# 512-column token products with four accumulators in two mixers of a transformer kernel

## The chip, the cores and the metric

The kernel runs on one core of a Trainium2 chip. The metric is the device time of one execution in microseconds (us), lower is better. A run's time is compared with runs of the kernel before on the same chip.

## What is computed

The reference is two transformer blocks on 512 tokens of width 1024, in float32. The first block is an FFN, a mixer (mixer 1) and a second FFN; the second is a mixer (mixer 2) and an FFN with a convolution. What the change touches are column ranges of the mixers' input products. Cut to these:

```
# mixer 1: h = rms_norm(x) [512, 1024]
c_q, k_a, v_a, k_idx, w_idx, q_b, k_b, v_b, gate_a, gate_b = split(h @ w_in)
y_b = stick_breaking_attention(q_b, k_b, v_b)     # 8 heads of 64: v_b has 512 columns
# mixer 2: u = rms_norm(h)
rq, rk, rv, rgate, dq, dk, dv, dz, db, da, gate_r, gate_d = split(u @ w_in_2)
rq, rk = rotary(rq), rotary(rk) / 8               # 512 columns each
ro  = retention_chunkwise(rq, rk, rv)             # rv, rgate: 1024 columns each
y_r = (silu(rgate) * group_norm(ro)) @ w_ret_br
do  = gated_delta_chunkwise(conv(dq), conv(dk), conv(dv), ...)
merged = sigmoid(gate_r) * y_r + sigmoid(gate_d) * (gated(do, dz) @ w_dn_br)
```

## The kernel before, in words

Every large product is three float32r products: both operands are cut into a high and a low part (`mm3`, L140: lines L143, L144, L145 are its three matmuls). `wpanel` (L126) loads a panel of weights by a DMA from SP's queue (L134), rounds it on ScalarE (L135, the high part) and subtracts on VectorE (L136, the low part). Four raw panels and two pairs of high and low panels exist at a time.

There are two shapes of product. `feat_gemm` (L155) has 128 weight columns as the stationary operand and streams 512 tokens: each matmul is 128x512. `tok_gemm` (L176) has 128 tokens as the stationary operand and streams the weight columns, 256 to 272 of them: each matmul is 128x256. For 256 columns it takes two panels of 4x256, and for each of four token blocks one accumulator after another: 8 x 3 matmuls into one PSUM bank, then the evacuation. So 256 columns are 4 x 24 = 96 matmuls.

PSUM has eight banks, divided by name and divided anew by `repsum` (L1488): `mm` is what both products use. In mixer 1's projections and in mixer 2 up to the first weave's end `mm` has 4 banks; in mixer 2's third weave 3; in its end 8. With 4 or more, `feat_gemm` takes 256 columns a step, otherwise 128.

**Mixer 1.** `b_proj` (L732) makes the stick attention's queries, keys and values for a half of the heads; the values (`e_v`, L756) are one `tok_gemm` of 256 columns a half. Half 0's values stay in two slots; half 1's go to DRAM by four DMAs (L761) and `b_stick` (L775) brings them back by two (L783). A slot is one of 45 SBUF buffers of 128x512 (`slot`, L46), given out when an older one is released.

**Mixer 2.** Retention's part: `proj_r(half)` (L1252) makes for a half of the heads queries and keys, 256 columns each, evacuated through `rope` (L490: on VectorE two products L495 and L496/L497 that read PSUM, a sum on GpSimd L502, a product L503) and values, twice 256 columns, evacuated by ScalarE (L1268). All go to DRAM (`stage`, L309) and come back in `ret_chain` (L1281). `ret_fin` (L1338) makes the gate, twice 256 columns a half: Silu on ScalarE (L1347), a product on GpSimd (L1348), four normalisations (L1352) and a product (L1354) on VectorE; then `to_features` transposes.

The rest of mixer 2: `dn_first`, `dn_rest` and `dn_fin` are the delta rule, a chain of small float32 products (for half 0 and half 1), `gates(br)` (L1363) the branch gates, 1024 columns each by `feat_gemm`, `merge` (L1371) the output products.

What sets the order: `weave` (L58) traces generators step by step side by side by weights, `urgent` (L70) moves steps up in priority by so many instructions, and a scheduler in the build puts each engine's instructions in order by these priorities and a simulated time. Each engine, and SP's DMA queue, then runs in that order. Mixer 2's order is written out in L1394 to L1411:

```python
    weave((urgent(C, dn_rest(0, d0), X1), 0.5), (urgent(C, dn_first(1, d1), X2), 1.0),
          (chain(proj_r(0, r0), gates(0)), 0.15))
    C.repsum({"mm": 3, "pd": 3, "pr": 2})
    weave((urgent(C, dn_rest(1, d1), X3), 0.75),
          (chain(dn_fin(0, d0), proj_r(1, r1), gates(1)), 1.0),
          (urgent(C, chain(ret_chain(0, r0), ret_fin(0, r0)), X4), 0.5))
```

The first of these two is called the second weave below, the other the third; in each the chain without `urgent` is the fill: products that wait for nothing and stand between the links of the delta rule's chain. A fourth weave has `ret_chain(1)` and the fill `dn_fin(1)` and seven steps of `merge(0)`; `ret_fin(1)`, the last step of `merge(0)` and `merge(1)` follow.

Of the kernel before, what the change touches and what calls it, by code (L numbers as in the profile page):

```python
# [8 lines left out]
F32 = mybir.dt.float32  # L9
# [3 lines left out]
OP = mybir.AluOpType  # L13
# [3 lines left out]
P = 128  # L17
# [10 lines left out]
class Ctx:  # L28
# [29 lines left out]
def weave(*gens):  # L58
    """Traces the generators' steps side by side; each is (generator, steps it takes for one of the others)."""
# [10 lines left out]
def urgent(C, g, offset):  # L70
    """g's steps, as if traced that many instructions earlier."""
# [38 lines left out]
def load_columns(C, rows, name, pool=None):  # L110
    """rows: APs [n, 128] in DRAM; returns a [128, sum n] tile with one column for each row."""
# [14 lines left out]
def wpanel(C, w, k0, nk, c0, n):  # L126
    """w[k0*128:(k0+nk)*128, c0:c0+n] as two float32r parts whose sum is exact."""
# [12 lines left out]
def mm3(C, ps, lhs, rhs, start, stop, **kw):  # L140
    """ps += lhs^T rhs from exact float32r parts: lhs and rhs are (hi, lo)."""
# [6 lines left out]
def split(C, src, hi, lo):  # L148
    """src = hi + lo, both float32r."""
# [5 lines left out]
def feat_gemm(C, h, w, kb, c0, ncols, evac, k0=0, tokens=T):  # L155
    """evac(j, psum) for each 128 columns of w: psum = (h w[k0*128:])^T, [128 columns, tokens]."""
# [19 lines left out]
def tok_gemm(C, h, w, kb, c0, n, evac):  # L176
    """evac(tb, psum): psum[:, :n] = (h w)[128 tokens of block tb, c0:c0+n]; n in 256..272, kb 8 or less."""
# [80 lines left out]
def rsqrt_small(C, src, n, scale, eps, name, bufs=2):  # L258
    """1/sqrt(src*scale + eps) on [128, n]: exp(-ln/2), then a Newton step."""
# [39 lines left out]
def spill(C, xT):  # L299
    """x goes to DRAM while the mixer needs its room."""  # L300
# [8 lines left out]
def stage(C, t, name):  # L309
    """A slot's content goes to DRAM for a while; unstage() brings it back."""  # L310
# [11 lines left out]
def add_spilled(C, xs):  # L322
    """The evacuation that adds to the x of spill(), and the list it fills with the sums."""
# [60 lines left out]
def ffn_conv(C, xT, g, wu, wd, cw, cb, last):  # L384
    """last(xT, G, f0) as in ffn_phases(); cw[tap], cb [128, 44]: taps and bias of the 44 blocks of 128 channels."""
# [50 lines left out]
def rope_setup(C, positions, inv_freq):  # L436
    """cos, sin [128 tok, 4 blocks, 32] of the positions' angles."""
# [36 lines left out]
def rope_table(C, cs, sn, g, scale, name):  # L474
    """ct, st [128, 4, 64]: rope(y*g)*scale = y*ct + halves_swapped(y)*st."""
# [14 lines left out]
def rope(C, out, src, ct, st, n, r=None, tag="ta"):  # L490
    """out [128, n, 64] = (src*ct + swap(src)*st) * r; ct, st broadcast to [128, n, 64]; r [128, n] or None."""
# [14 lines left out]
def mixer1(C, xT, a, W):  # L506
# [33 lines left out]
    yb, qa, qi, kT = [None] * 4, [], [None], []  # L540
# [4 lines left out]
    def a_proj():  # L545
        # c_q | k_a v_a k_idx w_idx, tokens on partitions
# [35 lines left out]
        # keys: norm, rope, and transposed twice over, for both halves of the partitions  # L582
# [18 lines left out]
        # queries  # L601
# [15 lines left out]
        def q_done(i, tb, src, r):  # L617
# [8 lines left out]
            # each head's two parts, on the two halves of the partitions  # L626
# [23 lines left out]
    def a_topk():  # L650
        # the index scores' 128 largest among the causal keys; block 0 has no more than 128
# [927 lines left out]
```

## Time and profile before

| | us |
|---|---|
| median of 3 runs | 2203.46 |
| the runs | 2199.79, 2203.46, 2204.78 |
| span of the profiled execution (first to last instruction; no other time is listed for it) | 2203.8 |
| TensorE busy in it | 2162.9 (98%) |
| VectorE, ScalarE, GpSimd busy | 1236.6, 900.5, 238.2 |

The page of the profile gives the busy time of each engine, the chain of work that ended last, and groups of instructions. Matmuls overlap in the pipeline, so a matmul's duration is longer than its distance to the next one; what one costs in a stream is the distance between starts, which is read from the rows in order of time.

### The profile page before, as it was taken

Reading aid. Unit: us, or ns where it says so; the run is one execution under the profiler, and the core shown is the slowest. Engines: PE = TensorE matmul, PEld = TensorE weight load, DVE = VectorE, ACT = ScalarE, POOL = GpSimd, SP = SyncE. Lnnn points to the kernel's source line nnn. Section 1 sums busy time; section 2 is a strip of 40 time slices with the busy share of each in tenths; the row PEclk is TensorE's granted clock in tenths of the full one; section 3 lists DMA queues with packets and bytes.
Section 4 is the critical chain, followed back from the end, with each engine's and each line's share of the span. In section 5 each row is a group of like instructions: output and inputs, shape, how many; then the busy total and the mean of one; then the engine's idle time right before and its main releaser. Section 6 shows DMA issues by size and latency. Waiting matters only on the chain.

```text
span 2203.8 us, 29456 instructions
## 1 busy us (share of the span) xinstructions
PE 2162.9 (98%) x11346; PEld 1837.3 (83%) x11346; DVE 1236.6 (56%) x2268; ACT 900.5 (41%) x1554; POOL 238.2 (11%) x221
## 2 busy tenths in 40 slices
PE   8999999999999899999999999999999999999998
PEld 6888888887887788888888889899888988888887
DVE  5542434578975744333446897654546455653662
ACT  4321223356578442212334545242344344432442
POOL 1110110114100001101100000011011110210210
PEclk9999999999999999999999999999999999999999
DMA  5333335578433833333243435533343452323331
GB/s 164 96 96 96 97 95 135 96 107 122 89 96 113 261 96 97 96 98 100 89 139 118 133 99 163 165 105 103 115 157 120 139 172 88 104 95 96 96 113 60
DMA packets 268206, 254.43 MB, mean 115 GB/s; under 512 B 25927, under 2 KB 237857, under 8 KB 268065
## 3 DMA queue, kind: packets, MB, share of 16 engines
q1 hardware_dynamic: 267488, 251.49, 40.4%
q8 instruction: 89, 1.46, 0.3%
q10 hardware_dynamic: 576, 1.05, 0.1%
q14 instruction: 53, 0.43, 0.1%
HBM read 221.02 MB, written 31.47 MB: 115 GB/s over the span
## 4 chain that ended last, share of the span: by engine, by line
PE 89%; DVE 3%; ACT 3%; DMA 3%; issue 1%; POOL 0%; SPq 0%; DVEq 0%; ACTq 0%; POOLq 0%
PE mm L145 27%; PE mm L144 27%; PE mm L143 26%; DVE wlo L136 1%; DMA tb<-part 1%; PE mm L720 1%; ACT whi L135 1%; DMA g<-t 1%; PE pb L838 1%; PE pb L799 1%; PE pd L1132 0%; PE pa L701 0%; PE pr L1313 0%; PE pb L828 0%; PE mm L717 0%
## 5 line engine op out<-in xcount | busy, mean ns | idle before, releaser
L143 PE MATMUL mm<-e,whi 128*128 128x512 f32 (+1 forms) x2240 | 865.3, 387 | 6.0 <-ACT e L150 3.2
L144 PE MATMUL mm<-e,whi 128*128 128x512 f32 (+1 forms) x2240 | 860.9, 385 | 0.0
L145 PE MATMUL mm<-e,wlo 128*128 128x512 f32 (+1 forms) x2240 | 832.2, 386 | 5.9 <-DVE wlo L136 5.8
L136 DVE TENSOR_TENSOR wlo<-raw,whi 128x1024 fp32r<-128x1024 f32 (+1 forms) x369 | 430.2, 1167 | 440.1 <-ACT whi L135 421.4
L135 ACT CAST whi<-raw 128x1024 fp32r<-128x1024 f32 (+1 forms) x369 | 369.4, 1002 | 693.7 <-PE mm L144 524.7
L143 PEld LDWEIGHTS mm<-e,whi 128*128 128x128 f32 x2240 | 420.9, 188 | 91.6 <-ACT e L150 4.4
L145 PEld LDWEIGHTS mm<-e,wlo 128*128 128x128 f32 x2240 | 420.7, 188 | 91.4 <-DVE wlo L136 9.2
L144 PEld LDWEIGHTS mm<-e,whi 128*128 128x128 f32 x2240 | 421.2, 188 | 83.7 <-issue 2.3
L144 PE MATMUL mm<-wlo,e 128*128 128x256 f32 (+3 forms) x672 | 194.5, 293 | 3.0 <-DVE wlo L136 2.9
L145 PE MATMUL mm<-whi,e 128*128 128x256 f32 (+3 forms) x672 | 193.6, 292 | 0.0
L143 PE MATMUL mm<-whi,e 128*128 128x256 f32 (+3 forms) x672 | 186.4, 292 | 3.1 <-ACT td L1233 1.8
L144 PEld LDWEIGHTS mm<-wlo,e 128*128 128x128 f32 x672 | 128.7, 192 | 6.2 <-DVE wlo L136 4.4
L368 POOL TENSOR_TENSOR t<-t,rb 128x512 f32<-128x512 f32 x44 | 65.4, 1487 | 616.2 <-ACT t L367 612.9
L143 PEld LDWEIGHTS mm<-whi,e 128*128 128x128 f32 x672 | 126.6, 192 | 6.4 <-ACT whi L135 2.0
L145 PEld LDWEIGHTS mm<-whi,e 128*128 128x128 f32 x672 | 128.6, 192 | 1.6
L396 DVE SCALAR_TENSOR_TENSOR t<-t,fcw 128x511 f32<-128x511 f32 x88 | 66.1, 751 | 29.0 <-ACT t L393 27.1
L411 POOL TENSOR_TENSOR t<-t 128x512 f32<-128x512 f32 x22 | 48.9, 2222 | 305.5 <-DVE t L396 280.6
L150 ACT CAST e<-t 128x512 fp32r<-128x512 f32 x50 | 31.0, 621 | 85.9 <-DVE t L375 43.4
L144 PE MATMUL mm<-g,whi 128*128 128x512 f32 x160 | 62.4, 390 | 0.0
L143 PE MATMUL mm<-g,whi 128*128 128x512 f32 x160 | 62.3, 390 | 0.0
L145 PE MATMUL mm<-g,wlo 128*128 128x512 f32 x160 | 60.1, 391 | 0.8 <-DVE wlo L136 0.8
L334 DVE SCALAR_TENSOR_TENSOR e<-mm,e 128x512 f32<-128x512 f32 x56 | 38.4, 689 | 37.2 <-PE mm L145 37.0
(408 smaller groups left out, 2249.8 us busy)
## 6 DMA issues: line engine op xcount, KB each, us to landing
raw<-w_in SPq DMA_DIRECT2D x100, 512.0 KB, 5.0
raw<-w_up SPq DMA_DIRECT2D x88, 512.0 KB, 3.7
raw<-w_down SPq DMA_DIRECT2D x59, 512.0 KB, 3.5
raw<-w_gate SPq DMA_DIRECT2D x44, 512.0 KB, 3.9
xs<-e SPq DMA_DIRECT2D x16, 256.0 KB, 3.3
g<-t SPq DMA_DIRECT2D x16, 256.0 KB, 2.0
raw<-w_o_a SPq DMA_DIRECT2D x16, 256.0 KB, 3.3
raw<-w_out SPq DMA_DIRECT2D x8, 512.0 KB, 8.4
```

Of the source, the lines that this page charges most:

```text
L135: nc.scalar.copy(hi[:, :N], raw[:, :N])
L136: nc.vector.tensor_tensor(lo[:, :N], raw[:, :N], fl(hi[:, :N]), op=OP.subtract)
L143: nc.tensor.matmul(ps, lhs[0], rhs[0], start=start, stop=False, **kw)
L144: nc.tensor.matmul(ps, lhs[0], rhs[1], start=False, stop=False, **kw)
L145: nc.tensor.matmul(ps, lhs[1], rhs[0], start=False, stop=stop, **kw)
L150: C.nc.scalar.copy(hi, src)
L334: C.nc.vector.scalar_tensor_tensor(xT[j], ps, alpha, xT[j], op0=OP.mult, op1=OP.add)
L368: nc.gpsimd.tensor_tensor(s3, s2, nm.rb, op=OP.mult)
L396: nc.vector.scalar_tensor_tensor(y[:, n:], u[:, :T - n], cw[k][:, f:f + 1], y[:, n:], op0=OP.mult, op1=OP.add)
L411: nc.gpsimd.tensor_tensor(pr, y, act[f + j], op=OP.mult)
L720: nc.tensor.matmul(po, va[:, sb, :], pp, start=sb == 0, stop=sb == tb)
L799: nc.tensor.matmul(zs(sb)[:, u * P:(u + 1) * P], k[:, sb * P:(sb + 1) * P], q[u][:, ts], start=(sb % 2 == 0 and u == 0), stop=False, skip_ ...
```

## The change

A second token product, `tok_gemm_wide`, streams 512 weight columns a matmul. It takes panels of 2x512 and four accumulators at once: each panel is used for all four token blocks (24 matmuls), and all four accumulators end within the last panel. It replaces `tok_gemm` in three places: the stick values of mixer 1 (one product of 512 columns in `b_proj(0)`, in four slots kept for both halves, with no way through DRAM), all of retention's queries, keys and values (`proj_r()` now makes both halves at once, four products), and the gate of half 1 (`ret_fin(1)`). `ret_fin(0)` keeps two products of 256.

The fill of mixer 2 changes with it: the second weave has all of `proj_r` and the first half (two steps of 256 columns) of `gates(0)`; the third has `dn_fin(0)`, the rest of `gates(0)` and `gates(1)`. `ret_chain` loads its half of queries and keys by eight DMAs of 128x256 and its values by four of 128x512, where eight of 128x512 stood.

The diff, cut to its core (removed comments and docstrings are left out):

```diff
+def tok_gemm_wide(C, h, w, kb, c0, evac):
+    acc = [ptile(C) for _ in range(4)]
+    for kp in range(0, kb, 2):
+        wp = wpanel(C, w, kp, 2, c0, 512)
+        for tb in range(4):
+            ts = slice(tb * P, (tb + 1) * P)
+            for k in range(2):
+                mm3(C, acc[tb], (h[0][kp + k][:, ts], h[1][kp + k][:, ts]), (wp[0][:, k, :], wp[1][:, k, :]),
+                    kp + k == 0, kp + k == kb - 1)
+            if kp + 2 == kb:
+                evac(tb, acc[tb])
+    yield
...
     def b_proj(half, st):
-        v = [C.dram.tile([P, T], F32, name=f"bsv{i}") if half else slot(C) for i in range(2)]
...
         def e_v(tb, ps):
-            cols = slice(tb % 2 * 256, tb % 2 * 256 + 256)
-            t = tmp(C)[:, :256] if half else v[tb // 2][:, cols]
-            nc.scalar.activation(t, ps[:, :256], AF.Copy, scale=nm.rt[:, tb:tb + 1])
-            if half:
-                nc.sync.dma_start(v[tb // 2][:, cols], t)
+            vb.append(slot(C))
+            nc.scalar.activation(vb[tb], ps, AF.Copy, scale=nm.rt[:, tb:tb + 1])
...
-        yield from tok_gemm(C, h, w_in, 8, 1544 + half * 256, 256, e_v)
+        if half == 0:
+            yield from tok_gemm_wide(C, h, w_in, 8, 1544, e_v)
...
-    def proj_r(half, st):
+    def proj_r():
+        def put(t, name, halves=2):
+            d = C.dram.tile([P, halves, T // halves], F32, name=name)
+            nc.sync.dma_start(d, t.rearrange("p (u n) -> p u n", u=halves))
+            return d
...
+                r = small(C, 8, "rdr", 3)
+                nc.vector.tensor_scalar(r, rdec[:, i, :], nm.rt[:, tb:tb + 1], None, op0=OP.mult)
+                w = lambda t: t.rearrange("p (h d) -> p h d", d=64)
+                t = slot(C)
+                rope(C, w(t), w(ps), rct[:, tb:tb + 1, :].to_broadcast([P, 8, 64]),
+                     rst[:, tb:tb + 1, :].to_broadcast([P, 8, 64]), 8, r, "td")
+                rkept[n].append(put(t, f"st{n}{tb}"))
...
+                t = slot(C)
+                nc.scalar.activation(t, ps, AF.Copy, scale=nm.rt[:, tb:tb + 1])
+                rkept[f"v{half}"].append(stage(C, t, f"stv{half}{tb}"))
...
+            yield from tok_gemm_wide(C, h, w_in, 8, i * 512, e_qk(n, i))
+        for half in range(2):
+            yield from tok_gemm_wide(C, h, w_in, 8, 1024 + half * 512, e_v(half))
...
     def ret_chain(half, st):
-        qk = {n: [unstage(C, d) for d in st[n]] for n in "qk"}
-        vv = [[unstage(C, d) for d in st[f"v{grp}"]] for grp in range(2)]
+        qk = {n: [slot(C), slot(C)] for n in "qk"}
+        for n in "qk":
+            for tb in range(4):
+                nc.sync.dma_start(tok(n, tb), rkept[n][tb][:, half, :])
+        vv = [unstage(C, d) for d in rkept[f"v{half}"]]
...
-        for grp in range(2):
-            yield from tok_gemm(C, h, w_in, 8, 2048 + half * 512 + grp * 256, 256, e(grp))
+        if half:
+            yield from tok_gemm_wide(C, h, w_in, 8, 2048 + half * 512, e(0, 512))
+        else:
+            for grp in range(2):
+                yield from tok_gemm(C, h, w_in, 8, 2048 + half * 512 + grp * 256, 256, e(grp))
...
-    m0 = merge(0)
+    m0, g0 = merge(0), gates(0)
...
-          (chain(proj_r(0, r0), gates(0)), 0.15))
+          (chain(proj_r(), some(g0, 2)), 0.15))
     C.repsum({"mm": 3, "pd": 3, "pr": 2})
     weave((urgent(C, dn_rest(1, d1), X3), 0.75),
-          (chain(dn_fin(0, d0), proj_r(1, r1), gates(1)), 1.0),
+          (chain(dn_fin(0, d0), g0, gates(1)), 1.0),
```

## Rows read from the trace of the kernel before

**Rows 1.** The page: span, TensorE's busy time, the chain that ended last.
```profile
span 2203.8 us, 29456 instructions
...
PE 2162.9 (98%) x11346; PEld 1837.3 (83%) x11346; DVE 1236.6 (56%) x2268; ACT 900.5 (41%) x1554; POOL 238.2 (11%) x221
...
PE 89%; DVE 3%; ACT 3%; DMA 3%; issue 1%; POOL 0%; SPq 0%; DVEq 0%; ACTq 0%; POOLq 0%
```

**Rows 2.** TensorE's groups by shape (busy us, mean ns, idle before): three of them.
```profile
L143 PE MATMUL mm<-e,whi 128*128 128x512 f32 x2112 | 827.3, 392 | 3.0 <-ACT e L150 2.0 <-ACT whi L135 1.0
...
L143 PE MATMUL mm<-whi,e 128*128 128x256 f32 x576 | 159.6, 288 | 2.2 <-ACT td L1233 1.8 <-ACT whi L135 0.4
...
L145 PE MATMUL mm<-whi,g 128*128 128x512 f32 x32 | 12.5, 390 | 0.0
```

**Rows 3.** TensorE in order of time (start us, us): end of mixer 2, gate of half 1.
```profile
1687.17 0.40 PE L144 MATMUL mm<-e,whi 128*128 128x512 f32 x1
...
1709.84 0.39 PE L145 MATMUL mm<-e,wlo 128*128 128x512 f32 x1
1710.07 0.28 PE L143 MATMUL mm<-whi,e 128*128 128x256 f32 x1
...
1721.46 0.28 PE L145 MATMUL mm<-whi,e 128*128 128x256 f32 x1
```

**Rows 4.** TensorE's waits over 150 ns from 1310 to 1550 us (total, times, longest).
```profile
PE mm L144 <- DVE wlo L136: 1.4, 3, 0.7
...
PE mm L143 <- ACT whi L135: 0.4, 1, 0.4
```

**Rows 5.** VectorE and GpSimd by shape: the rope's instructions, mixer 1, eight heads.
```profile
L503 DVE TENSOR_TENSOR ta<-ta,rq 128x512 f32<-128x512 f32 x4 | 2.8, 693 | 0.8 <-POOL ta L502 0.6
...
L495 DVE TENSOR_TENSOR ta<-pa,tic 128x512 f32<-128x512 f32 x3 | 2.1, 692 | 6.1 <-PE pa L145 6.1
...
L496 DVE TENSOR_TENSOR ta<-pa,tis 128x256 f32<-128x256 f32 x3 | 1.2, 415 | 0.0
...
L502 POOL TENSOR_TENSOR ta<-ta 128x512 f32<-128x512 f32 x4 | 6.0, 1504 | 25.7 <-DVE ta L497 25.7
```

**Rows 6.** VectorE by shape, 1310 to 1550 us: the panel splits.
```profile
L136 DVE TENSOR_TENSOR wlo<-raw,whi 128x1024 fp32r<-128x1024 f32 x30 | 36.6, 1220 | 16.6 <-DMA e<-ret_norm_g 9.4 <-ACT whi L135 7.0
```

**Rows 7.** Busy time by stretch: us, PE, PEld, DVE, ACT, POOL, clock, DMA.
```profile
1310.00:1450.00 140.00, 137.70 (x1009) 126.11 (x1008) 99.69 (x270) 55.48 (x153) 9.97 (x17) 1.00 0.53 155
1450.00:1640.00 190.00, 187.62 (x1386) 174.16 (x1385) 96.16 (x223) 65.71 (x122) 24.01 (x30) 1.00 0.39 118
```

**Rows 8.** ScalarE by shape: a copy of 512 columns out of PSUM.
```profile
L639 ACT COPY ya<-pa 128x512 f32<-128x512 f32 x4 | 2.3, 583 | 1.1 <-PE pa L145 1.1
```

**Rows 9.** The delta rule's first and last product by half (first to last start).
```profile
L1124 PE MATMUL pd<-dw x32: 271/275/347, 1322.9 to 1399.9; 128*128 128x128 f32 x32
...
L1180 PE MATMUL pd<-td,dw x32: 270/275/276, 1367.3 to 1444.5; 128*128 128x128 f32 x32
...
L1124 PE MATMUL pd<-dw x32: 273/275/276, 1458.4 to 1588.9; 128*128 128x128 f32 x32
...
L1180 PE MATMUL pd<-td,dw x32: 270/275/276, 1551.2 to 1641.9; 128*128 128x128 f32 x32
```

**Rows 10.** TensorE in order of time around its longest wait in mixer 2.
```profile
1651.18 0.39 PE L143 MATMUL mm<-whi,e 128*128 128x256 f32 x1 [1.77 <-ACT td L1233]
...
1652.49 0.42 PE L145 MATMUL mm<-whi,e 128*128 128x256 f32 x1
1652.70 0.42 PE L143 MATMUL mm<-whi,e 128*128 128x256 f32 x1
```

**Rows 11.** Busy time by stretch, same columns as rows 7: the same place.
```profile
1651.00:1654.50 3.50, 3.32 (x18) 3.32 (x19) 2.47 (x6) 1.77 (x4) 2.62 (x4) 0.63 0.00 0
```

**Rows 12.** SP's DMA issues in order of time: loads of half 1's stick.
```profile
517.50 0.81 SPq L318 DMA_DIRECT2D e<-bsk  x2
...
524.06 2.39 SPq L318 DMA_DIRECT2D e<-bsv  x2
```

More of the change, by code (lines that the diff above doesn't have):

```diff
@@ L775, in b_stick @@
     def b_stick(half, st):
-        q, k, v = st["q"], st["k"], st["v"]
+        q, k = st["q"], st["k"]
         if half:
@@ L782, in b_stick @@
                     nc.sync.dma_start(q[-1][u][hd_rows(u)], d[hd_rows(u)])
-            k, v = [unstage(C, d) for d in k], [unstage(C, d) for d in v]
-        v = [t.rearrange("p (b n) -> p b n", b=2) for t in v]
+            k = [unstage(C, d) for d in k]
         yb[half * 2:half * 2 + 2] = [pc.tile([P, T], F32, name=f"yb{half}{i}") for i in range(2)]
@@ L787, in b_stick, with stick @@
             for pp in range(2):
-                yield from stick(half * 2 + pp, tb, q[pp], k[pp], v, slice(pp * P, (pp + 1) * P))
+                yield from stick(half * 2 + pp, tb, q[pp], k[pp])
                 done[half] += 1
-    def stick(pr, tb, q, k, v, vs):
+    def stick(pr, tb, q, k):
         nb = tb + 1
@@ L837, in stick @@
             c_ = slice((sb % 2) * 256, (sb % 2) * 256 + 256)
-            nc.tensor.matmul(py[:, :256], v[sb // 2][:, sb % 2, vs], am[sb // 2][:, c_], start=sb == 0,
+            nc.tensor.matmul(py[:, :256], vb[sb][:, pr * P:(pr + 1) * P], am[sb // 2][:, c_], start=sb == 0,
                              stop=sb == nb - 1)
@@ L999, in mixer2 @@
     ro, rT = [None] * 8, [None] * 8
+    rkept = {"q": [], "k": [], "v0": [], "v1": []}
     def proj_d(half, st):
@@ L1250, in dn_fin @@
         yield
-    def proj_r(half, st):
-        qk = {}
-        tok = lambda n, tb: qk[n][tb // 2][:, (tb % 2) * 256:(tb % 2) * 256 + 256]
-        put = lambda n, ts: [stage(C, t, f"st{n}{half}{i}") for i, t in enumerate(ts)]
+    def proj_r():
[3 more added lines that the diff above has]
+            return d
         def e_qk(n, i):
             def e(tb, ps):
-                r = small(C, 4, "rdr", 3)
-                nc.vector.tensor_scalar(r, rdec[:, i, half * 4:half * 4 + 4], nm.rt[:, tb:tb + 1], None, op0=OP.mult)
-                w = lambda t: t[:, :256].rearrange("p (h d) -> p h d", d=64)
-                rope(C, w(tok(n, tb)), w(ps), rct[:, tb:tb + 1, :].to_broadcast([P, 4, 64]),
-                     rst[:, tb:tb + 1, :].to_broadcast([P, 4, 64]), 4, r, "td")
+                r = small(C, 8, "rdr", 3)
[5 more added lines that the diff above has]
+                rkept[n].append(put(t, f"st{n}{tb}"))
@@ L1264, in e_qk, with e_v @@
             return e
-        def e_v(grp):
+        def e_v(half):
             def e(tb, ps):
-                nc.scalar.activation(v[tb // 2][:, (tb % 2) * 256:(tb % 2) * 256 + 256], ps[:, :256], AF.Copy,
-                                     scale=nm.rt[:, tb:tb + 1])
+                t = slot(C)
+                nc.scalar.activation(t, ps, AF.Copy, scale=nm.rt[:, tb:tb + 1])
+                rkept[f"v{half}"].append(stage(C, t, f"stv{half}{tb}"))
             return e
         for i, n in enumerate("qk"):
-            qk[n] = [slot(C), slot(C)]
-            yield from tok_gemm(C, h, w_in, 8, i * 512 + half * 256, 256, e_qk(n, i))
-            st[n] = put(n, qk[n])
@@ L1275, in proj_r @@
-        for grp in range(2):
-            v = [slot(C), slot(C)]
-            yield from tok_gemm(C, h, w_in, 8, 1024 + half * 512 + grp * 256, 256, e_v(grp))
-            st[f"v{grp}"] = put(f"v{grp}", v)
+            yield from tok_gemm_wide(C, h, w_in, 8, i * 512, e_qk(n, i))
+        for half in range(2):
+            yield from tok_gemm_wide(C, h, w_in, 8, 1024 + half * 512, e_v(half))
         yield
     def ret_chain(half, st):
-        qk = {n: [unstage(C, d) for d in st[n]] for n in "qk"}
@@ L1341, in ret_fin, with e @@
                                       ap=[[0, P], [1, 512]]))
-        def e(grp):
+        def e(grp, n=256):
             def f(tb, ps):
-                cols = slice(grp * 256, grp * 256 + 256)
+                cols = slice(grp * 256, grp * 256 + n)
                 z1, z2 = tr(), tr()
-                nc.scalar.activation(z1[:, :256], ps[:, :256], AF.Silu, scale=nm.rt[:, tb:tb + 1])
-                nc.gpsimd.tensor_tensor(z2[:, :256], z1[:, :256], gr[:, cols], op=OP.mult)
+                nc.scalar.activation(z1[:, :n], ps[:, :n], AF.Silu, scale=nm.rt[:, tb:tb + 1])
+                nc.gpsimd.tensor_tensor(z2[:, :n], z1[:, :n], gr[:, cols], op=OP.mult)
                 o = ro[half * 4 + tb]
-                for hh in (grp * 2, grp * 2 + 1):
+                for hh in range(grp * 2, grp * 2 + n // P):
                     i = tb * 4 + hh
@@ L1353, in f @@
                                             op0=OP.subtract, op1=OP.mult)
-                nc.vector.tensor_tensor(o[:, cols], o[:, cols], z2[:, :256], op=OP.mult)
+                nc.vector.tensor_tensor(o[:, cols], o[:, cols], z2[:, :n], op=OP.mult)
             return f
-        for grp in range(2):
-            yield from tok_gemm(C, h, w_in, 8, 2048 + half * 512 + grp * 256, 256, e(grp))
+        if half:
[3 more added lines that the diff above has]
+                yield from tok_gemm(C, h, w_in, 8, 2048 + half * 512 + grp * 256, 256, e(grp))
         to_features(ro, rT, half, tr)
```

6 lines of the change are left out of this document (3 added, 3 removed).

## The prediction

> **What bounds the kernel now.** I read the page first. TensorE is busy 98% of the span and holds 89% of the chain that ended last, and its granted clock is 1.00 in the stretches looked at, the 2.4 GHz level, but for one place below [rows 1, 7]. So the time is what TensorE's stream costs, plus its few waits; VectorE, ScalarE and the DMA queues count only where they make it wait. Next I read its groups by shape [rows 2]: nearly all is the three lines of the split product, in two shapes, 128x512 and 128x256. The durations there (392 and 288 ns) are not costs: they overlap. What one matmul costs is the distance between starts, and one place shows both shapes side by side [rows 3]. From 1687.17 to 1709.84 us there are 100 steps of 128x512: 22.67/100 = 0.2267 us. From 1710.07 to 1721.46 us there are 95 steps of 128x256: 11.39/95 = 0.1199 us. Twice the columns cost less than twice the time. Then the waits [rows 4] and the chains around the fill [rows 7, 9].
>
> **Term 1, the pitch.** Replaced are products of 256 columns, 96 matmuls each: two for the stick values, eight in retention's queries, keys and values, two in the gate of half 1. That is 12 x 96 = 1152 narrow matmuls, and 576 wide ones for the same columns. A pair of narrow ones costs 2 x 0.1199 = 0.2398 us, a wide one 0.2267, so 0.0131 us is saved a pair: 576 x 0.0131 = **-7.5 us**. All of it lies on the path, since TensorE is the path. By rounding of the rows the pitch is good to 0.0002 us, so this term is -7.3 to -7.8 if the streams run without waits. The Trainium skill, page "TensorE: Matmul & The Clock Gate", section "Back-to-back issue gap", gives a gap that is nearly proportional to the columns (262 cycles for 256, 518 for 512); by it a pair would save 6 cycles, 2.5 ns at 2.4 GHz, and the whole change 1.4 us. The trace does not agree with that: its rows have 13 ns a pair, in an undisturbed stretch.
>
> **Term 2, waits of the narrow products.** A narrow product holds both pairs of panels to its last token block, so the next one's panel (a rounding on ScalarE, then 1.22 us on VectorE [rows 6]) is late. From 1310 to 1550 us, where `proj_r` runs, these waits are 1.4 + 0.4 us [rows 4]. A wide product uses a panel for 24 matmuls, 24 x 0.2267 = 5.4 us, and lets it go; a panel's 1.22 us fits. I take -1.0, with 0 and -1.8 as ends.
>
> **Term 3, the evacuation of queries and keys.** All four accumulators end within one panel, 6 x 0.2267 = 1.36 us apart, and they are all of `mm`. No row before has this. The next product's first matmul on a bank comes 5.4 us after the last one of the product before. VectorE must by then have read the bank: three reads of eight heads, 0.69 and twice 0.42, 1.5 us [rows 5] (the small product of the factors is left aside), and it has 0.69 more for the last step when GpSimd's 1.50 is through [rows 5]. Four banks are 4 x 2.2 = 8.8 us of VectorE; the fourth bank's reads end 3 x 2.2 + 1.5 = 8.1 us after the first bank ended, and are wanted at 3 x 1.36 + 5.4 = 9.5. So with VectorE to itself nothing waits; but it is busy 99.69 of 140 us there [rows 7]. Some of that is the narrow rope, which the wide one replaces, the rest panel splits and the delta rule's work. If the rest takes two fifths, 8.1 becomes 8.1/0.6 = 13.5, and the fourth bank is 4 us late. This happens at two borders (queries to keys, keys to values); the values go by ScalarE copies of 0.58 us [rows 8], faster than 1.36. Ends: 0 and 2 x 4 = +8. The delta rule's products of the second weave can stand in the hole, as they use other banks, so I take +1.0 a border: **+2.0**.
>
> **Term 4, the gate of half 1.** Its four accumulators too end together. ScalarE's Silu (0.58, as the copy in [rows 8]), GpSimd's product (1.50, as the sum of that size in [rows 5]) and VectorE's product (0.69) follow each: the first Silu is through 3.5 us before the last matmul ends, GpSimd's four products 4 x 1.5 later, 2.5 us after that end, VectorE's some 3 us after it. The cover is the last step of `merge(0)`, 48 x 0.2267 = 10.9 us, and the first panel of `merge(1)`, which wants only half 0. I take 0; without the cover it is +3.
>
> **Term 5, the fill in another place.** The second weave gets 384 x 0.2267 = 87.1 us of `proj_r` for 384 x 0.1199 = 46.0, and gives up half of a gate, 96 x 0.2267 = 21.8: +19.3 us. The third gives up 46.0 and gets 21.8: -24.2. The sum is the -5 of term 1 that belongs to `proj_r`; the move itself costs nothing as long as TensorE has work in both. VectorE and ScalarE get fewer, longer instructions, DMA six transfers fewer in mixer 1 and eight more loads in mixer 2, all hidden behind four raw panels; a store of queries that waits for the rope holds SP's queue, and with it the next panel, for some 9 to 14 us, where four panels last 4 x 5.4 us. If that cover were gone, one panel wait of a few us would follow. I take 0. The ends come from one event: at 1651 us TensorE waited 1.77 us for a Silu, and then ran at a lower granted clock, 0.63 over 3.5 us, the narrow pitch going to 0.21 us (the 1.2 GHz level) [rows 10, 11]; some 19 matmuls at 0.21 instead of 0.12 are 1.7 us, so 3.5 us for the event. The new order may lose it or make another: -3.5 to +3.5.
>
> **The sum:** -7.5 - 1.0 + 2.0 = -6.5 us. The profiled span, 2203.8 us, is 0.3 above the median of the three runs, 2203.46, so the two are taken as one: 2203.5 - 6.5 = **2197.0 us**. The runs lie 5 us apart; 0.2% (4.4 us) is about what a measurement of this kernel can tell from no change.
>
> **The rivals.**
>
> *More than forecast.* The borders cost nothing because the delta rule fills them, and the wait at 1651 us does not come again: -7.5 - 1.8 - 3.5, near 2191 us. For it: VectorE has less to do in the rope. Against: the fourth weave, where that wait lies, is the same. 15%.
>
> *The four banks.* Both borders cost their full 4 us: -7.5 - 1 + 8, near 2203 us, within 0.2%. For it: VectorE's 71% in that stretch. Against: the delta rule's products. It shows as waits of L143 on the rope or on L1268. The Trainium skill's "Perfetto Trace Analysis", section "Matmuls" under "Optimizing Tensor Performance", asks that groups rotate through PSUM banks so that one's evacuation overlaps the next one's matmuls. The narrow products do that and their evacuations appear in none of the waits of that stretch [rows 4], so the trace agrees as far as it goes; the wide ones give the rotation up. 19%.
>
> *Mixer 1's slots.* Half 0 now holds four value slots instead of two, until the sticks end. The second stick's keys come at 517.5 us, its values at 524.1 [rows 12], each when a slot comes free. If the keys come as late as the values now do, that stick starts 6.6 us later; if the mixer's end moves with it, -6.5 + 6.6, 2203.5 us. Against: gate products fill TensorE meanwhile. 6%.
>
> *The other side: the third weave runs dry.* The delta rule's half 1 goes from its first product at 1458.4 to its last decay product at 1641.9, 183.5 us [rows 9]. If that is the chain's own length, taking 24.2 us of fill out of the third weave saves nothing there, while the second weave grows by 19.3: 2203.5 + 19.3 - 2.5 (the stick and gate products), 2220 us; already half of it is 2208, slower. It decides once the chain needs over 159 us. Against it: half 0 did the same from 1322.9 to 1444.5, 122 us, beside as much other work [rows 9]. 8%.
>
> *The change doesn't do what it says*: a wide matmul among token-major weights costs more than a token-major one of `feat_gemm`, so that two narrow ones are as cheap. Against: the kernel's last product has that form already, and its row shows 390 ns beside 392 [rows 2]. 2%; 2203 us.
>
> **The numbers.** The forecast itself gets 50%, 2194 to 2199. Faster by over 0.2% are the forecast and the first rival: 0.65. Within 0.2%: banks, slots and the last rival, 0.27. Slower: 0.08. The range reaches from short of the first rival's end to the bank rival's, 2190 to 2204.5, and leaves out the dry weave and the tails.
>
> **What would show it.** Right: 576 fewer matmuls; L143 to L145 at 128x256 down from 576 to 192 each, wide pitch 0.227 us in `proj_r`; no waits of L144 on the low panel there; few waits on rope lines. Wrong: several us of waits of `mm` on L495 to L497 at two borders near 1340 and 1365 us; waits of `pd` or `pr` products and idle TensorE from 1460 to 1640 us; or falls of the granted clock in more than one place.

## The result and the profile after

The changed kernel takes 2224.26 us (median of 4 runs, 2223.59 to 2225.78), the kernel before on the same chip 2204.03 (4 runs): ratio 1.0096, 95% interval 1.0082 to 1.0111. It is 20 us slower; forecast was 6.5 us faster. The page of the changed kernel:

```profile
span 2224.1 us, 28228 instructions
...
PE 2165.3 (97%) x10770; PEld 1812.8 (82%) x10770; DVE 1238.2 (56%) x2224; ACT 898.8 (40%) x1538; POOL 237.2 (11%) x209
...
PEclk9999999989999999999999999999999999999999
```

The 576 matmuls are gone [rows 1], yet TensorE is busy 2.4 us longer, and its granted clock shows an 8 in the ninth slice, from 445 to 500 us. TensorE in order of time (start, us, and in brackets the wait before) shows what happens there, and two other places:

```profile
481.34 1.03 PE L640 MATMUL pa<-ident,ta 128*128 128x128 f32 x8
486.60 0.66 PE L640 MATMUL pa<-ident,ta 128*128 128x128 f32 x4 [4.23 <-DVE ta L518]
490.13 1.09 PE L640 MATMUL pa<-ident,ta 128*128 128x128 f32 x4 [2.87 <-DVE ta L518]
...
494.96 0.76 PE L143 MATMUL mm<-e,whi 128*128 128x512 f32 x1 [1.62 <-DVE e L646]
495.53 0.63 PE L144 MATMUL mm<-e,whi 128*128 128x512 f32 x1
495.95 0.63 PE L145 MATMUL mm<-e,wlo 128*128 128x512 f32 x1
...
549.20 2.04 PE L810 MATMUL pb<-e 128*128 128x128 f32 x8 [6.26 <-DMA e<-bsk]
550.89 0.77 PE L144 MATMUL mm<-e,whi 128*128 128x512 f32 x1
...
1174.09 0.39 PE L144 MATMUL mm<-wlo,e 128*128 128x272 f32 x1 [0.82 <-DVE wlo L136]
...
1729.70 0.39 PE L143 MATMUL mm<-whi,e 128*128 128x512 f32 x1
...
1751.23 0.39 PE L145 MATMUL mm<-whi,e 128*128 128x512 f32 x1
```

The wait at 1174.09 is a landmark: a token product in mixer 2's first projections, ahead of everything in mixer 2 that the change touches. In the kernel before the same wait of 0.82 us stands here:

```profile
1152.23 0.39 PE L144 MATMUL mm<-wlo,e 128*128 128x272 f32 x1 [0.82 <-DVE wlo L136]
```

So 21.9 us are lost before mixer 2 and 1.6 won behind it. All of the loss is in mixer 1, where the change replaced two products of 256 columns by one of 512, a step that the forecast priced at little over 1 us of gain. It lies in two places. At 481 to 495 us the last query transposes of mixer 1's other attention (L640, before L625) wait for their ropes with nothing beside them: call it the dry end. At 549 us the stick's score product (L810, before L799) waits for the second stick's keys. The four waits of these two places are 4.23 + 2.87 + 1.62 + 6.26 = 15.0 us. From 340 to 1120 us TensorE's listed waits (over 150 ns) sum to 30.7 us here and to 15.7 in the kernel before, so the two places hold all the added waiting. What more was lost, 6.9 us, goes with the clock: behind each wait TensorE runs slower. Busy time by stretch (columns as in rows 7), after:

```profile
482.00:502.40 20.40, 11.69 (x45) 9.57 (x44) 14.11 (x24) 8.29 (x19) 2.93 (x3) 0.67 0.37 72
...
543.20:556.80 13.60, 7.60 (x31) 6.59 (x32) 4.09 (x6) 5.70 (x12) 2.63 (x3) 0.75 0.58 134
```

and before:

```profile
482.00:502.40 20.40, 20.00 (x110) 17.04 (x109) 15.68 (x36) 14.71 (x29) 8.26 (x10) 1.00 0.81 148
...
543.20:556.80 13.60, 12.41 (x63) 9.82 (x63) 12.48 (x29) 11.39 (x24) 8.13 (x9) 1.00 0.41 85
```

The granted clock is 0.67 and 0.75 where it was 1.00; at 495.53 and 495.95 us wide matmuls stand 0.42 us apart, nearly twice the 0.2267 of rows 3, the 1.2 GHz level. SP's DMA issues tell why both come late. After:

```profile
390.77 27.32 SPq L134 DMA_DIRECT2D raw<-w_in  x6
422.86 0.37 SPq L620 DMA_DIRECT2D raw<-w_uq_a  x1
...
506.80 1.44 SPq L794 DMA_DIRECT2D e<-bsq  x2
...
530.22 1.09 SPq L794 DMA_DIRECT2D e<-bsq  x2
...
536.80 3.38 SPq L333 DMA_DIRECT2D e<-bsk  x1
...
541.22 2.82 SPq L333 DMA_DIRECT2D e<-bsk  x1
```

Before:

```profile
390.38 18.84 SPq L134 DMA_DIRECT2D raw<-w_in  x4
411.73 0.37 SPq L605 DMA_DIRECT2D raw<-w_uq_a  x1
...
494.95 4.13 SPq L782 DMA_DIRECT2D e<-bsq  x4
```

The query weights (`w_uq_a`) are issued 11.1 us later, behind six panels instead of four. The second stick's queries (`bsq`) go out in two pairs 23 us apart instead of four at once, and its keys (`bsk`) follow at 536.80 and 541.22, where they were at 517.50 [rows 12]. Each of these loads needs a free slot, and SP's queue runs in order. The queue's own waits show it. After, from 490 to 550 us:

```profile
SPq L794 <- PE pa L673: 6.5, 1, 6.5
```

Before:

```profile
SPq L318 <- PE pa L658: 6.5, 1, 6.5
```

L673 and L658 are the same product of the other attention in the two kernels. In the kernel before the stick's keys wait for it (L318, issued at 517.50 us); in the changed one the second pair of queries does (L794, issued at 530.22 us), and the keys stand behind those.

### The profile page after: what moved, and what is told of

It reads as the page before. It is cut to its first block, busy times and chain, and to the rows that moved or that the text cites. A ratio compares the mean times of both kernels' runs of the same rounds, so it can differ in the third digit from the quotient of the medians.

```text
span 2224.1 us, 28228 instructions
## 1 busy us (share of the span) xinstructions
PE 2165.3 (97%) x10770; PEld 1812.8 (82%) x10770; DVE 1238.2 (56%) x2224; ACT 898.8 (40%) x1538; POOL 237.2 (11%) x209
## 4 chain that ended last, share of the span: by engine, by line
PE 90%; DVE 4%; ACT 3%; DMA 2%; issue 1%; POOL 0%; SPq 0%; DVEq 0%; ACTq 0%; POOLq 0%
PE mm L145 27%; PE mm L144 27%; PE mm L143 27%; DVE wlo L136 1%; ACT whi L135 1%; PE pb L810 1%; PE mm L735 1%; DMA tb<-part 1%; PE pb L849 1%; DMA e<-bsk 1%; PE pa L716 0%; PE pd L1144 0%; PE pa L673 0%; PE pd L1187 0%; PE pb L839 0%
## 5 line engine op out<-in xcount | busy, mean ns | idle before, releaser
L143 PE MATMUL mm<-e,whi 128*128 128x512 f32 (+1 forms) x2240 | 866.4, 388 | 11.1 <-ACT e L150 5.0
L144 PE MATMUL mm<-wlo,e 128*128 128x512 f32 (+3 forms) x480 | 161.3, 338 | 1.6 <-DVE wlo L136 1.5
L145 PE MATMUL mm<-whi,e 128*128 128x512 f32 (+3 forms) x480 | 160.7, 337 | 0.0
L143 PE MATMUL mm<-whi,e 128*128 128x512 f32 (+3 forms) x480 | 151.0, 338 | 4.9 <-ACT td L1245 3.3
L143 PEld LDWEIGHTS mm<-whi,e 128*128 128x128 f32 x480 | 90.5, 190 | 15.3 <-ACT td L1245 3.7
L144 PEld LDWEIGHTS mm<-wlo,e 128*128 128x128 f32 x480 | 91.3, 191 | 11.6 <-DVE wlo L136 2.8
L145 PEld LDWEIGHTS mm<-whi,e 128*128 128x128 f32 x480 | 91.2, 190 | 8.5
```

The source lines that it names most:

```text
L143: nc.tensor.matmul(ps, lhs[0], rhs[0], start=start, stop=False, **kw)
L144: nc.tensor.matmul(ps, lhs[0], rhs[1], start=False, stop=False, **kw)
L145: nc.tensor.matmul(ps, lhs[1], rhs[0], start=False, stop=stop, **kw)
```

## The experiments

Sixteen kernels, in the order of their runs. Each is set against runs of the kernel before on its own chip (2201.0 to 2201.7 us); brackets give the 95% interval of the ratio. The edits are cut to their core, and `...` and `[...]` stand for what is left out.

**m2_only.** The changed kernel with mixer 1 as before (`e_v`, `b_proj`, `b_stick` of the diff undone).

> The changed kernel with mixer 1's stick values as in the kernel before (two narrow products, half 1's values through DRAM); mixer 2 as changed. Theory A (the loss is all in mixer 1, where the trace after shows 8.7 us of waits of the query ropes' transposes at 482 to 493 us and 6.3 us for the second stick's keys at 542 us, each followed by the 1.2 GHz level): 2201 to 2204 us, no waits over 3 us before 760 us, since from mixer 2's start to the end the kernel after is only 1.6 us shorter than before. Rival B (the third weave runs dry, the prediction's rival on the other side): stays near 2220 us, with idle TensorE between the second and third weave.

2202.01 us, ratio 1.0002 [0.9992, 1.0012]. The loss is not in mixer 2. But its gain does not show either. Its longest waits from 1150 to 1900 us:

```profile
PE mm L143 <- ACT td L1249: 3.3, 1, 3.3
PE pd L1191 <- DVE td L1187: 1.5, 1, 1.5
PE mm L143 <- DVE e L349: 1.4, 1, 1.4
...
PE mm L1243 <- DVE dw L1375: 1.0, 1, 1.0
```

**m1_only.** The counterpart: the kernel before with mixer 1's part of the change alone.

> The kernel before with mixer 1's part of the change alone (one product of 512 columns for the stick values, four slots). Theory A: near 2225 us, 21 to 22 us over the kernel before, with the same two waits at 482 to 493 and 542 us. Rival B: 2202 us, the pitch's 1.3 us saved and nothing else.

2222.97, ratio 1.0098 [1.0077, 1.0118], with waits of 6.6 us in sum on L625's counterpart and 6.0 on `e<-bsk`. Mixer 1's part is the whole loss.

**uq_early.**
```diff
+        w_uq = [...]        # load and split of w_uq_a, w_q_idx
         for i, tab in enumerate((tk, ti)):
...
-        w_uq = [...]
```

> The changed kernel with the load and split of the two query weights traced two steps earlier in a_proj; SP then issues them before the wide product's four panels instead of behind them, and nothing else moves on SP. Theory A1 (the query chain starts 11 us late because its weights stand behind the four panels on SP's queue, so that its last ropes come when the fill is used up): the waits at 482 to 493 us and the 13.65 us at the 1.2 GHz level that follow go, some 13 us less, near 2211 us; the wait for the second stick's keys stays. Rival C (the chain is late because the four value slots leave its queries no slots): 2224 us as the changed kernel.

2219.86, ratio 1.0083 [1.0063, 1.0104]. The wait on the last transposes falls from 7.1 to 2.1 us, but the one behind it (on L646) grows from 1.6 to 2.8, a panel is 2.4 us late near 407 us, and the wait on `e<-bsk` stays (6.2). The gain is about 3 of the 13 us that the theory had, which is between theory and rival.

**values_last.**
```diff
-        if half == 0:
+        if half == 1:
             yield from tok_gemm_wide(C, h, w_in, 8, 1544, e_v)
```

> The changed kernel with the wide value product in b_proj's second half, where half 1's narrow one stood, so that it is the last of the fill; the slots and everything else as changed. Theory A1: the query ropes are covered again and the query weights' load is no longer behind its panels: 12 to 14 us less, 2210 to 2212 us, if the second stick's keys still wait 6 us for their slots; 2203 to 2206 if that wait goes too. Rival C: 2224 us, as the slots are as many as in the changed kernel when the queries are made.

2222.26, ratio 1.0094 [1.0074, 1.0115]: a miss. The waits on the last transposes are gone, but the first product behind the projections (L673), in PSUM divided anew, then waits 5.2 us for the values' ScalarE copies (L772), which still hold its banks. One dry end was exchanged for another; `e<-bsk` stays.

**values_staged.** The wide product stays beside half 0; half 1's 256 columns go to DRAM and come back, so two slots are held instead of four.
```diff
-            vb.append(slot(C))
-            nc.scalar.activation(vb[tb], ps, AF.Copy, scale=nm.rt[:, tb:tb + 1])
+            cols = slice(tb % 2 * 256, tb % 2 * 256 + 256)
+            if tb % 2 == 0:
+                vb.append(slot(C))
+            t = tmp(C)[:, :256]
+            nc.scalar.activation(vb[tb // 2][:, cols], ps[:, :256], AF.Copy, scale=nm.rt[:, tb:tb + 1])
+            nc.scalar.activation(t, ps[:, 256:], AF.Copy, scale=nm.rt[:, tb:tb + 1])
+            nc.sync.dma_start(vd[tb // 2][:, cols], t)
```

> The changed kernel, wide value product still beside half 0, but half 1's 256 value columns go to DRAM and come back as before, so that two value slots are held instead of four. Theory (slots make the second stick's keys late, and the first product on them then waits about 6 us and lowers the clock): the wait of the stick's score product on e<-bsk and the half-rate stretch near 545 us are gone, the wait of the last query transposes near 485 us stays; about 10 us less than the changed kernel, near 2211 against 2201 for the kernel before on its chip. Rival (what is late is the projections, and the keys follow them): the wait on e<-bsk stays, 2220 to 2224.

2212.56 against 2201.65, ratio 1.0047 [1.0031, 1.0063], as the theory had it. No wait on `e<-bsk` is left, the dry end stays. In SP's DMA issues all four query loads go together again:

```profile
505.51 2.91 SPq L800 DMA_DIRECT2D e<-bsq  x4
...
529.00 0.81 SPq L333 DMA_DIRECT2D e<-bsk  x2
```

Its longest wait of TensorE in mixer 1 (total, times, longest):

```profile
PE pa L641 <- DVE ta L518: 6.4, 2, 4.0
```

**last_staged.** values_last with that edit.

> The wide value product stands beside half 1, where the narrow one of half 1 stood, and half 1's 256 columns go through DRAM, so both suspected costs are taken away at once. Theory (two costs of about 10 us each, the last queries without cover and the slots): no wait over 2 us on the last query transposes nor on e<-bsk, no half-rate stretch between 480 and 550 us; about 2200, the time before or a few us less. Rival (half 0's stick now has its values too late, or the new accumulators of the last transposes wait for the evacuation of the four wide ones): a wait of 5 us on the values or on that bank, 2208 to 2214.

2210.66, ratio 1.0041 [1.0026, 1.0056]. No wait on `e<-bsk`; 5.6 us on the copies. The rival for the banks held.

**uq_staged.** uq_early with that edit.

> The changed kernel with the load of the query weights traced ahead of the keys' loop (so it stands in SP's queue ahead of the wide product's panels) and with half 1's values through DRAM. Theory (two costs): the two savings add, no wait over 3 us on the last query transposes nor on e<-bsk; 2202 to 2207, since the early load itself costs a panel wait near 407 us. Rival (the second cost is not the slots): as with the early load alone, 2218 to 2221.

2209.47, ratio 1.0034 [1.0020, 1.0049]. The savings add, but less than forecast: waits of 2.1 us on the last transposes and 1.8 behind them remain, and one of 2.1 on a panel near 407.

**narrow_kept.** The reverse test of the slots: m2_only, whose products in mixer 1 are narrow and where they were, with half 1's values kept in two slots.
```diff
-        v = [C.dram.tile([P, T], F32, name=f"bsv{i}") if half else slot(C) for i in range(2)]
+        v = [slot(C) for i in range(2)]
```

> The kernel before in mixer 1's products (two narrow value products, at their old places), mixer 2 as changed, but half 1's values stay in two slots instead of going through DRAM: four value slots held, nothing else of mixer 1 changed. Theory (the slots alone delay the keys): a wait of some us on e<-bsk and a half-rate stretch behind it, 2206 to 2212. Rival (four slots don't matter, the wide product's early place does): no such wait, 2201 to 2203.

2210.3, ratio 1.0042 [1.0030, 1.0054], against 1.0002 without the edit. It shows the same picture as the changed kernel. (`e_v` then writes both halves' values straight into slots, and `b_stick` loads none.) SP's DMA issues:

```profile
497.00 1.15 SPq L795 DMA_DIRECT2D e<-bsq  x2
...
519.25 1.09 SPq L795 DMA_DIRECT2D e<-bsq  x2
...
525.84 0.86 SPq L333 DMA_DIRECT2D e<-bsk  x1
```

TensorE's longest wait in mixer 1:

```profile
PE pb L812 <- DMA e<-bsk: 5.7, 1, 5.7
```

The busy time of the stretch around it (columns as in rows 7):

```profile
530.00:544.00 14.00, 8.35 (x32) 6.85 (x31) 4.98 (x11) 6.48 (x13) 1.95 (x2) 0.76 0.66 128
```

The stretch idles 14.0 - 8.35 = 5.65 us. A clock of 0.76 over it is at most 0.24 x 14.0 = 3.4 us more, at most 9.0 together; it is less as far as the clock was already low within the wait. Measured are 8.8 (0.0040 x 2201), good to some 3 us by the two intervals.

**m2_balanced.** m2_only with half 1's values as two narrow products in the third weave (the wide form doesn't fit there: `mm` has three banks). The new argument of `proj_r` tells whether it makes those values or all the rest.
```diff
-          (chain(proj_r(), some(g0, 2)), 0.15))
+          (chain(proj_r(False), some(g0, 2)), 0.15))
...
-          (chain(dn_fin(0, d0), g0, gates(1)), 1.0),
+          (chain(dn_fin(0, d0), proj_r(True), g0, gates(1)), 1.0),
```

> Mixer 1 as in the kernel before; mixer 2 as changed, but the values of half 1 are again two narrow products and stand in the third weave, so that the second and third weave have as much fill as before (87 and 44 us). The changed mixer 2 alone gave 2202.0 against 2201.0, though the pitch should save 6.3. Theory (the third weave is short of fill): the waits near 1461 us (2.4 us and a fall of the clock) are gone, 5.0 us of pitch stay saved: 2196 to 2198 against about 2201.5 of its chip. Rival (the gain goes elsewhere, to the waits at the ends of the fourth weave and of the gate): the wait near 1644 us stays 3.3 us, 2200 to 2202.

2212.83, ratio 1.0047 [1.0030, 1.0064]: 10 us worse than m2_only and outside both forecasts. Now the second weave runs dry. TensorE waits 3.0 us at 1427 us in the delta rule's inversion (L1146), and runs at the lower clock for most of the 20 us that follow. The wait, from TensorE's waits in mixer 2:

```profile
PE pd L1146 <- DVE td L1141: 3.0, 1, 3.0
```

The busy time of the 20 us behind it:

```profile
1429.00:1449.00 20.00, 17.68 (x96) 15.75 (x96) 10.96 (x38) 4.59 (x16) 1.05 (x2) 0.57 0.27 81
```

**m2_starved.** The opposite: `chain(proj_r(), g0)` in the second weave, no gate of branch 0 in the third.

> Mixer 1 as before; mixer 2 as changed, but all of the first branch's gate stands in the second weave, so the third one loses another 21.8 us of fill. Theory (the third weave is short of fill): the waits between 1440 and 1640 us grow to 5 us or more, and the total by 4 to 22 us, 2206 to 2222. Rival (the chain of the third weave keeps up): no new waits there, 2200 to 2203.

2205.99, ratio 1.0021 [1.0011, 1.0032], 4 us over m2_only, at the theory's low end. The waits near 1461 us are gone; others stand at the third weave's end, from 1637 to 1650 us (retention's loads 1.7 and 1.4, its chain 3.3, a Silu 2.7).

**cover_staged.** uq_staged with `some(g0, 2)` for `some(g0, 0)` in mixer 1: two steps of its gate ahead of the second pool, that is, before PSUM is divided anew for the sticks.

> The kernel with the early load of the query weights and half 1's values through DRAM (2209.5 against 2201.7), with two steps of mixer 1's gate moved ahead of the second pool, behind half 1's keys, where the narrow value product used to stand. Theory (what is left are the last queries' ropes without cover): the waits near 485 and 490 us (2.1 us each) and the fall of the clock behind them are gone, 2202 to 2205. Rival (the gate is then missing under the sticks, or its evacuation holds the banks of the new pool): waits elsewhere, 2207 to 2211.

2228.42, ratio 1.0123 [1.0108, 1.0138]. The waits near 485 us are gone, but 19 us are lost later, in many waits of up to 2.2 us each and at a lower granted clock (0.88 from 520 to 540 us). That is slower than both forecasts. It goes with the rival, by which the gate is then missing beside the sticks; no run takes this apart.

**early_narrow.** The kernel before, with half 1's narrow value product directly behind half 0's, where the wide one stands.
```diff
-        yield from tok_gemm(C, h, w_in, 8, 1544 + half * 256, 256, e_v)
+        if half == 0:
+            for u in range(2):
+                yield from tok_gemm(C, h, w_in, 8, 1544 + u * 256, 256, e_v(u))
```

> The kernel before (mixer 2 too), with one edit: half 1's narrow value product stands directly behind half 0's, where the wide one stands in the changed kernel; still 128x256, one bank after another, half 1's columns through DRAM, two value slots. Theory (the place of half 1's values is the second cost: the last queries' ropes lose their cover): waits of 4 to 8 us on the last query transposes near 485 us and a half-rate stretch behind them, 2208 to 2213 against about 2201.5. Rival (the wide form is the cost: four accumulators and four panels of 512 columns at a time): no such wait, 2200 to 2203.

2200.27 against 2201.01, ratio 0.9994 [0.9984, 1.0003]. The rival held, and a theory fell. The place of half 1's values costs nothing; the last transposes are covered by half 1's queries and keys as well as they were by its values. What costs in that place is the wide form with what comes with it.

**steps_staged.** A weave counts steps, and `tok_gemm_wide` is one step of 96 wide matmuls where two narrow products were two steps of half the time. So: values_staged, and
```diff
+        if halves and kp == 2:
+            yield
```

> The changed kernel with half 1's values through DRAM (2212.6 against 2201.7 before), and one edit more: the wide value product of mixer 1 gives way to the query chain in its middle, so that it counts as two steps of the weave, as two narrow ones did. Theory (the step of double length is the second cost): the load of the query weights is issued near 412 us again, no wait over 2 us on the last query transposes, no half-rate stretch near 485 us; 2199 to 2202. Rival (the wide form itself: four accumulators, four panels): the waits near 485 us stay, 2208 to 2213.

2220.66, ratio 1.0088 [1.0073, 1.0103]: a miss to the other side. The load of `w_uq_a` is back at 412 us, but now the four accumulators' copies stand behind the whole query chain in ScalarE's order. ScalarE in order of time:

```profile
453.87 1.05 ACT L135 CAST whi<-raw 128x1024 fp32r<-128x1024 f32 x1 [3.66 <-PE mm L145]
...
478.37 0.58 ACT L648 CAST e<-pa 64x512 fp32r<-64x512 f32 x1 [0.75 <-DVE e L649]
478.98 0.47 ACT L778 ACTIVATE e<-mm,rt 128x256 f32<-128x256 f32 x1
...
481.49 0.52 ACT L779 ACTIVATE t<-mm,rt 128x256 f32<-128x256 f32 x1
```

The busy time of that stretch:

```profile
455.00:485.00 30.00, 14.17 (x49) 10.50 (x48) 19.99 (x35) 13.89 (x28) 5.05 (x4) 0.62 0.32 38
```

The wide product's last matmul starts at 453.40 us, the copies run at 479 to 482 us (L778, L779). Until then all four banks of `mm` are held. TensorE's longest waits in mixer 1:

```profile
PE pa L643 <- DVE ta L520: 13.0, 4, 6.0
...
PE mm L143 <- ACT t L779: 2.9, 1, 2.9
```

The last transposes (L643) wait for their ropes with nothing beside them, and the first product of the fill stands behind them in TensorE's order and waits for the copies. TensorE idles 16 of 30 us, at a granted clock of 0.62.

**steps_only.** The changed kernel with that `yield` alone.

> The changed kernel with nothing but the wide value product of mixer 1 in two steps; four value slots are held. Theory (two causes, step length and slots): the 13.65 us at half rate near 485 us are gone, the wait on e<-bsk and its half-rate stretch stay; 2208 to 2212. Rival (the step length does nothing): 2220 to 2224.

2230.92, ratio 1.0134 [1.0114, 1.0155]: slower than both forecasts, with the same dry stretch and 6.2 us on `e<-bsk`.

**all_steps.** steps_staged with the `yield` in every wide product.

> As the kernel with half 1's values through DRAM and mixer 1's wide product in two steps, and every wide product of mixer 2 in two steps as well. Theory (the double step costs mixer 2 its pitch too): the waits near 1461 and 1645 us shrink, 3 to 6 us less than the kernel without it, 2194 to 2198. Rival (mixer 2 loses it elsewhere): within 2 us of that kernel.

2231.39, ratio 1.0135 [1.0118, 1.0152], some 10 us slower than steps_staged, where the theory had 3 to 6 us less and the rival no change. Its profiled execution has new waits for the inversion in mixer 2 (4.2 us); it took 2240.27 us, 8 to 10 us longer than the others, so these waits may be more than the usual.

**uq_mid.** values_staged, with the load and split of the query weights traced inside the wide product.
```diff
             if kp + 2 == kb:
                 evac(tb, acc[tb])
+        if hook and kp == 2:
+            hook()          # load_uq()
```

> The changed kernel with half 1's values through DRAM (2212.6 against 2201.7), and the load and split of the query weights traced between the second and the third panel of the wide value product, so that SP issues it near 412 us as in the kernel before; nothing else moves. Theory (the late load is the second cost): the first query product near 428 us, no wait over 2 us on the last query transposes, 2201 to 2205. Rival (the wide matmuls between the links of the query chain): the links stay 9 us apart, waits of 2 us and more near 485 us stay, 2207 to 2211.

2207.25, ratio 1.0024 [1.0013, 1.0035], at the rival's low end. The load is at 412 us again, and half of what values_staged lost is gone. SP's issue:

```profile
412.26 0.37 SPq L752 DMA_DIRECT2D raw<-w_uq_a  x1
```

Two of TensorE's longest waits in mixer 1:

```profile
PE mm L734 <- ACT ta L733: 3.2, 2, 2.6
...
PE pa L639 <- DVE ta L520: 2.1, 1, 2.1
```

The first query product starts at 428.7 us (427.3 in the kernel before, 436.6 in the changed one). The next two links of its chain, transposes of L639, follow 8.8 and 9.1 us apart where it was 7.1 and 6.7: in TensorE's order 32 wide matmuls stand between them, 32 x 0.2267 = 7.3 us, where 47 and 41 narrow ones took 5.6 and 4.9. The chain, 1.4 us late at its first product, is 5.4 us late behind these two links and 4.6 us at its last transposes (485.19 us, 480.57 before).

A larger pool of slots was not tried.

## Why the prediction was wrong

**The step that failed is mixer 1's value product.** The forecast counted its columns in the pitch (96 pairs of term 1's 576, 1.3 us of gain), put everything else of it into one rival of 6%, and had no term for what the new product moves in the queues. Three effects were left out or priced wrong:

*The slots* (the rival "mixer 1's slots"). The mechanism was named rightly, the price and the chance were not. The forecast said 6.6 us, and against it "gate products fill TensorE meanwhile". They don't: TensorE runs in a fixed order, and once L810 stands first in it, the gate behind it waits too (the row at 550.89 us). With the lower clock behind the wait the price is about 10 us. Five pairs of kernels that differ in where half 1's values are kept, in slots or in DRAM (with the copies and transfers that this takes), show it: 0.0049 of 2201 us (changed kernel and values_staged), 0.0053 (values_last and last_staged), 0.0049 (uq_early and uq_staged), 0.0040 (m2_only and narrow_kept), 0.0046 (steps_only and steps_staged), 8.8 to 11.7 us, each good to 3 to 6 us by the intervals. narrow_kept shows it without any wide product in mixer 1.

*The panels ahead of the query weights' load.* The forecast counted "DMA six transfers fewer in mixer 1" as hidden and did not ask what is queued behind the four panels that the wide step issues at once. From values_staged to uq_mid that is 0.0023, some 5 us; the two intervals overlap a little, so the size is rough. Two other pairs, changed kernel and uq_early, values_staged and uq_staged, have 0.0013 each, with a panel that comes late instead.

*The wide matmuls between the query chain's links.* What is left, 0.0024 or 5 us, goes with the links that stay 9 us apart. This is read from the order of TensorE's work; no run takes it alone away, and uq_mid has waits later in mixer 1 that may belong to something else.

0.0049 + 0.0023 + 0.0024 = 0.0096 is the whole ratio, but the sum proves nothing, since the last term is what the other two leave. The first is shown, the second is shown with a rough size, and the cause of the third stays open.

**Term 1, the pitch, was right.** From 1729.70 to 1751.23 us the changed kernel has 95 steps of the wide token-major matmul: 21.53/95 = 0.2266 us, forecast 0.2267, in 128x512 with tokens as weights. The rival "the change doesn't do what it says" falls with it. The Trainium skill, page "TensorE: Matmul & The Clock Gate", section "Back-to-back issue gap", gives 518 cycles for 512 columns, 0.216 us at 2.4 GHz, for a matmul by itself; the row, from a stream, is 5% above that, and the measurement decides.

**Term 2, the narrow products' panel waits, was right.** From 1310 to 1550 us 1.4 + 0.4 us were waited for panels [rows 4]; after, of the same view:

```profile
PE pd L1187 <- DVE td L1183: 1.5, 1, 1.5
PE pd L1192 <- DVE td L1189: 0.8, 1, 0.8
PE mm L143 <- ACT whi L135: 0.7, 1, 0.7
```

That is 1.1 us less.

**Term 3, the four banks at two borders, was too high.** No wait on a rope line stands in that view, where waits over 150 ns are listed, so it costs nothing there. But the mechanism exists. In steps_staged, with ScalarE in VectorE's part and behind a chain instead of beside one, the four banks are held for some 25 us and TensorE idles 16 of 30. The Trainium skill's "Perfetto Trace Analysis", section "Matmuls" under "Optimizing Tensor Performance", asks that groups rotate through PSUM banks; the traces agree where the evacuation is queued late, and not at the borders of `proj_r`.

**Term 4, the gate, was forecast at 0** because the last step of `merge(0)` and the first panel of `merge(1)` would cover the evacuation. They don't stand there: behind the gate's last matmul at 1751.23 us TensorE's next row is the gate's transposes at 1752.59, which wait 0.97 us for VectorE's product. That is less than the 3 us forecast without cover, but little of the gate's 1.3 us of pitch is left.

**Term 5, the moved fill, was forecast at 0 with 3.5 either way.** The event at 1651 us came again, at 1670.81 us in the changed kernel, with 3.3 us of waiting instead of 1.77 [rows 10]. In the third weave new waits of 1.5 and 0.8 us for the delta rule stand near 1487 us. So the rival "the third weave runs dry" came true in a small way: a few us of waits, not 20. m2_starved and m2_balanced show how narrow the room is: 21.8 us of fill moved out of the third weave cost 4 us, about as much moved out of the second 10. Forecast for mixer 2 were 5.3 us of gain (480 pairs of pitch 6.3, panels 1.0, borders -2.0); m2_only's interval allows at most 0.0008, 1.8 us. Its waits of 3.3 (1.77 before), 1.5, 1.4 and 1.0 us are all new or longer. From 1150 to 1900 us its listed waits sum to 12.5 us, those of the kernel before to 8.7: 3.8 more where terms 2 and 3 had 1.0. A granted clock of 0.97 from 1430 to 1480 us adds at most 1.5, so 6.3 - 3.8 - 1.5 = 1.0 us of gain is left, within that interval.

No version was found that beats the kernel before by more than a measurement can tell; early_narrow is level with it.

## What to carry to other kernels

When TensorE is the path and each engine runs in a fixed order, a longer product is not only cheaper columns: it issues its panels at once, holds all its banks at once and keeps its results in memory for longer, so write down for each of these what stands behind it on SP, on the evacuating engine and in the pool. "Other work fills the gap" holds only for work that stands ahead of the waiting instruction in that engine's order. And price a wait of several us on TensorE with the lower clock that follows it: at most 3.4 us with a wait of 5.7 in narrow_kept, and at most 0.43 x 20 = 8.6 us behind one of 3.0 in m2_balanced.

## What was not expected of the hardware

The stretch at the lower clock was longer than the wait that it went with. With levels of 1.00 and 0.50, a mean of 0.76 over 14 us is 6.7 us at the lower one; it went with a single wait of 5.7 us in narrow_kept, in part within it. In the changed kernel waits of 4.23, 2.87 and 1.62 us within 14 us go with 0.67 over 20.4 us, 13.5 us at the lower level, and the wide pitch was still 0.42 us when TensorE had work again. In m2_balanced a single wait of 3.0 us, in a stretch where TensorE had only the delta rule's small products, was followed by 20 us at 0.57, 17.2 us at the lower level, and m2_balanced is 10 us slower than m2_only. After the wait of 1.77 us in the kernel before it was 0.63 over 3.5 us, 2.6 us at the lower level [rows 10, 11].
